# A two-layer diffusion backbone: earlier first weights, convolution reads at another priority, square sums through PSUM

## The chip, the cores and the metric

The kernel runs on one core of one Trainium2 chip. The metric is the device time of one execution in microseconds (us), as the median of several runs. TensorE (PE) multiplies, VectorE (DVE), ScalarE (ACT) and GpSimd (POOL) do the rest, and SyncE (SP) issues the transfers from and to HBM. Matrix products land in PSUM, in banks of 128 partitions x 512 fp32 numbers; everything else lives in SBUF.

## The reference, cut to what matters

The latent stream `x` has 512 tokens, the context 256, each token 1024 numbers; there are two layers. Each layer normalises its input, modulates it by a condition (`w_ada`), sends it through four mixers side by side, merges these, and ends with a SwiGLU FFN. The context is written out by the first layer only.

```python
mod_l = (silu_c @ w_ada[l] + b_ada[l])[:, None, :]
sh1, sc1, g1, sh2, sc2, g2 = jnp.split(mod_l, 6, axis=-1)
h_lat = modulate(rms_norm(x, norm1_g[l]), sh1, sc1)
h_ctx = modulate(rms_norm(h_ctx_stream, norm1_g[l]), csh1, csc1)
p_lat = h_lat @ lp['w_in']      # S5, SGU, SSD, latent attention, gates
p_ctx = h_ctx @ lp['w_in']
...
# latent attention: the low-rank q (384) and kv (256) are normalised per token
q = rms_norm(cq, lp['mla_q_a_norm']) @ lp['mla_w_uq']
kv = rms_norm(ckv, lp['mla_kv_a_norm']) @ lp['mla_w_ukv']
...
# SSD: a centred depthwise convolution of three taps over the tokens, then silu
xbc = jax.nn.silu(conv_centred(xbc, lp['ssd_conv_w'], lp['ssd_conv_b']))
...
x = x + g1 * mix_lat
x = x + g2 * swiglu(modulate(rms_norm(x, norm2_g[l]), sh2, sc2), w_ffn_in[l], w_ffn_out[l])
```

## The kernel before

Activations lie transposed: 128 features on the partitions, tokens along the row (768: 256 of the context, `CTXS`, and 512 latent, `LAT`). A product in fp32 is made of three products of halves: `split` lets ACT round a value to its high half (`whi`, `xh`, `hh`) and POOL or VectorE subtract to get the low half (`wlo`, `xl`, `hl`), and `mm3` multiplies high by low, high by high and low by high into one bank. `weights` loads 256 columns of a matrix by one transfer into a `raw` tile and splits them 128 at a time; there are two buffers each of `raw`, `whi` and `wlo`. `proj` takes such a pair of weights, runs the eight blocks of 128 features (24 products for one segment) into an `acc` bank, of which there are two, and hands the bank to a callback that reads it on ACT or VectorE.

*The start.* `run` issues the transfers for `x`, then by `ada_first` those for the first eight chunks of the modulation: 16 tiles `h` of 384 KB and 8 tiles `f` of 256 KB (the last quarter), then the context, then the first weights of `w_in` (`first = next(ws)`, with the casts). It transposes the latent tokens, norms them, multiplies the modulation chunks (`ada_chunk`: products with the condition `cT`, a copy `gs`, a transpose, a sum), and lets `norm_mod` write `h` for the latent tokens. `next(xt)` transposes the context, the second `next(norm)` norms it: squares on ACT, their sum on VectorE, a product with `ones` that sums over the features, a reciprocal root in about ten small steps on VectorE, a product that spreads the result over the partitions, and the modulated `h` of the context. Then `params_more` and `s5_scalars` prepare small parameters. `mix` begins with two projections (128 columns each of q's low-rank part): both over the latent tokens, then both over the context.

*The heads.* `mla_pair` handles 256 tokens of q (three blocks of features, `nk` = 3) or kv (`nk` = 2): load, split, the squares on ACT into an SBUF tile `sc`, their sum by one or two adds on VectorE, then `tok_rsqrt` (the product with `ones`, four instructions of 128 columns for 256 tokens, and a root), the products of the heads, a norm of each head and its rotation, and transposes (`b<-k,g`). It runs eleven times, six in layer 0 and five in layer 1, beside generators of the state-space layer.

*The convolution.* A callback of `conv` reads a bank three times: ACT multiplies by the middle tap, VectorE adds the two neighbours by two `scalar_tensor_tensor` instructions. It runs within `fill`, between the steps of attention.

*What sets the order.* Nobody writes an engine's order out: a scheduler sorts the instructions of all engines by priority, which is the order of the program shifted by `high_priority(offset)`, by data and by free buffers. `at(fill, -1000)` puts the projections of `fill` 1000 places back, `five` runs 300 ahead. Each engine then works its own queue strictly in that order, and so does SP's for its transfers. PSUM's eight banks are `acc` (2), `b1` (4) and `b5` (2); both of the last are called `b` in the rows. The helpers give the lines: L169 and L171 are ACT, L174 `tensor_tensor` on VectorE or POOL, L186 and L190 VectorE, L193 a product, L197 a transpose, L481 a copy.

Of the kernel before, what the change touches and what calls it, by code (L numbers as in the profile page):

```python
# [13 lines left out]
AF = mybir.ActivationFunctionType  # L14
ALU = mybir.AluOpType
# [4 lines left out]
P = 128  # L20
# [6 lines left out]
BR = 384  # L27
# [13 lines left out]
C_CQ = 2188  # L41
# [44 lines left out]
class Net:  # L86
# [311 lines left out]

    def ada_first(s, l):

        src = s.t["w_ada"][l].rearrange("(k p) f -> p k f", p=P)
        out = []
        for pool, tag, c, w, cuts in ((s.hp, "h", 0, 768, (0, 512, 768)), (s.hp, "h", 768, 768, (0, 256, 768)), (s.fp, "f", 1536, 512, (0, 512))):
            rows = []
            for k in range(KD):
                raw = pool.tile([P, w], F32, tag=tag, name=s.nm(tag))
                s.dma.dma_start(out=raw, in_=src[:, k, c:c + w])
                rows.append(raw)
            for a, b in zip(cuts, cuts[1:]):
                out.append(((c + a) // 256, b - a, [x[:, a:b] for x in rows]))  # L410
        return out

# [234 lines left out]
    def mla_pair(s, part, q, kd, off, t0, b0, xd, nk, nw, wh, wl, qk):  # L647
# [7 lines left out]
        s.split(xh, xl, x)  # L655
        sq, z = s.sc(), s.sc()
        s.act(sq, x[:, 0:2].rearrange("p k t -> p (k t)"), AF.Square)
        s.add(sq[:, :256], sq[:, :256], sq[:, 256:])
        if nk == 3:
            s.act(z[:, :256], x[:, 2], AF.Square)  # L660
            s.add(sq[:, :256], sq[:, :256], z[:, :256])
        r = s.tok_rsqrt(sq, 2, 1.0 / (nk * P), eps)
# [621 lines left out]

    def mix(s, l, q, xs, xd, hh, hl, segs, rest, ws):

# [13 lines left out]
        def to_dram(d, segs_, f=None):  # L1300
            y = s.gs()

            def cb(ps, off, n, v):
                (f or s.act)(y[:, off:off + n], ps)
                if off == segs_[-1][0]:
                    s.spill(d[:, off:], y[:, off:])
            return cb
# [11 lines left out]
        ws = ws or s.weights(w_in, C_CQ, BR)  # L1319
        pair = [(next(ws), to_dram(dq[c * P:(c + 1) * P], segs)) for c in range(2)]  # L1320
        for sg in segs:
            for w, cb in pair:
                s.proj(w, hh, hl, [sg], cb)
        s.proj(next(ws), hh, hl, segs, to_dram(dq[2 * P:BR], segs))
        next(load, None)
# [52 lines left out]
        def conv(c, segs_):  # L1378
# [3 lines left out]
            def cb(ps, off, n, v):  # L1382
                a = y[:, off:off + n]
                s.act(a, ps, AF.Identity, scale=w(1), bias=q["cb"][:, c:c + 1])
                s.stt(a[:, 1:n], ps[:, 0:n - 1], w(0), a[:, 1:n], ALU.mult, ALU.add)
                s.stt(a[:, 0:n - 1], ps[:, 1:n], w(2), a[:, 0:n - 1], ALU.mult, ALU.add)
                z = s.sc()[:, :n]
# [74 lines left out]

    def layer(s, l, q, f, xs, hh, hl, xd, extra, rest, late, then, ws=None):
        full = l < DEPTH - 1
        segs = [LAT, CTXS] if full else [LAT]
        yd, gd = s.mix(l, q, xs, xd, hh, hl, segs, rest, ws)
        mh, ml = s.merge(l, yd, gd, segs)
# [71 lines left out]
    def run(s):  # L1539
# [3 lines left out]
        xr = s.load_x()  # L1543
        chunks = s.ada_first(0)
        xr = s.load_ctx() + xr
        ws = s.weights(s.t["w_in"][0], C_CQ, BR)
        first = next(ws)
        q = turn({})
# [32 lines left out]
        next(norm)  # L1581
        next(xt)
        next(norm)
        s.params_more(0, q)
        L8 = 21
        s.s5_scalars()
        ex = prepare()
# [9 lines left out]

        s.layer(0, q, a["f"], xs, hh, hl, xd, ex, rest(a, 8, L8), rest(a, L8, 24), then, chain([first], ws))
        xd = [s.dram(f"x1_{k}", [P, TOK]) for k in range(KD)]
# [34 lines left out]
```

## Time and profile before

| | us |
|---|---|
| median of 3 runs | 2734.05 |
| lowest, highest | 2726.58, 2735.45 |
| the profiled execution | 2746.22 |
| its span in the trace | 2744.4 |
| TensorE busy | 2614.2 |
| VectorE, POOL, ACT busy | 1390.6, 1217.3, 959.9 |
| mean granted clock of TensorE, of 1 | 0.978 |

The profile is of one execution. The page begins with each engine's busy time, and goes on with slices of the span, the costliest groups of instructions, and what an engine's idle time was ended by. A table of stretches gives the same for any piece of the span, with the clock that TensorE was granted: 1.00 is 2.4 GHz, 0.50 is 1.2 GHz. The list in order of time shows single instructions, with the idle time before them in brackets and the instruction that ended it.

### The profile page before, as it was taken

The numbers are of one execution on the slowest core, as the hardware profiler recorded it, in microseconds if no ns is written. First come the engines' busy times: TensorE is split into PE (matmuls) and PEld (weight loads), VectorE is DVE, ScalarE is ACT, GpSimd is POOL, SyncE is SP. The second block draws the span as 40 slices with busy tenths as digits, with TensorE's granted clock in tenths as the row PEclk, the third lists the DMA queues.
The fourth block names the chain that finished last, engine by engine and source line by source line (L and its number), as shares of the span: only waits on it lengthen the run. The fifth ranks groups of instructions, "written<-read, shape, count | busy, mean of one in ns | idle before, by whom it ended". The sixth has DMA issues, their size and how long they took to land. (4 is left out here: it accounts for less than half of the span.)

```text
span 2744.4 us, 39887 instructions
## 1 busy us (share of the span) xinstructions
PE 2614.2 (95%) x14964; PEld 2136.0 (78%) x14964; DVE 1390.6 (51%) x2944; ACT 959.9 (35%) x1901; POOL 1217.3 (44%) x877
## 2 busy tenths in 40 slices
PE   7998999998999989999999989999999999899999
PEld 4787777777888877888888877887766877678887
DVE  6667777656535666552221243666647454421111
ACT  4244455552222233222222234445543233322222
POOL 3255544424433746563423334543224545444443
PEclk9999999999999999999999999999999999899999
DMA  7656645644446553442321334665544565333332
GB/s 254 179 177 196 193 149 164 193 124 149 141 145 215 174 164 118 119 123 71 100 78 55 100 103 156 195 194 179 154 145 151 183 191 188 92 111 93 101 99 77
DMA packets 426039, 397.31 MB, mean 145 GB/s; under 512 B 53092, under 2 KB 372248, under 8 KB 425752
## 3 DMA queue, kind: packets, MB, share of 16 engines
q1 hardware_dynamic: 425848, 394.78, 46.4%
q8 instruction: 118, 1.93, 0.3%
q14 instruction: 73, 0.60, 0.1%
HBM read 305.66 MB, written 89.05 MB: 144 GB/s over the span
## 5 line engine op out<-in xcount | busy, mean ns | idle before, releaser
L174 POOL TENSOR_TENSOR wlo<-raw,whi 128x1024 fp32r<-128x1024 f32 (+2 forms) x314 | 630.1, 2008 | 1040.9 <-ACT whi L169 995.4
L193 PE MATMUL acc<-h,whi 128*128 128x512 f32 (+2 forms) x3496 | 1043.4, 368 | 14.3 <-DVE gs L186 6.7
L193 PE MATMUL acc<-h,wlo 128*128 128x512 f32 (+2 forms) x2060 | 760.1, 369 | 11.7 <-POOL wlo L174 6.5
L193 PEld LDWEIGHTS acc<-h,whi 128*128 128x128 f32 (+1 forms) x3496 | 625.1, 190 | 127.8 <-issue 15.4
L169 ACT CAST whi<-raw 128x1024 fp32r<-128x1024 f32 (+2 forms) x390 | 324.9, 834 | 759.7 <-PE b L193 319.4
L193 PEld LDWEIGHTS acc<-h,wlo 128*128 128x128 f32 (+1 forms) x2060 | 390.9, 190 | 83.7 <-POOL wlo L174 11.7
L193 PE MATMUL acc<-g,whi 128*128 128x512 f32 (+1 forms) x768 | 244.8, 390 | 13.2 <-DVE g L186 6.3
L193 PE MATMUL acc<-f,whi 128*128 128x512 f32 (+1 forms) x600 | 230.6, 394 | 6.4 <-POOL f L174 6.1
L193 PE MATMUL b<-h,whi 128*128 128x256 f32 (+1 forms) x696 | 220.8, 326 | 0.0
L193 PE MATMUL b<-h,wlo 128*128 128x256 f32 (+1 forms) x660 | 216.1, 327 | 3.0 <-POOL wlo L174 3.0
L193 PE MATMUL b<-g,whi 128*128 128x256 f32 (+1 forms) x768 | 197.3, 334 | 1.9 <-ACT whi L169 1.9
L193 PE MATMUL b<-f,whi 128*128 128x256 f32 (+1 forms) x600 | 186.6, 321 | 1.7 <-ACT whi L169 1.7
L193 PE MATMUL b<-g,g 128*64 128x128 f32 (+5 forms) x915 | 183.7, 354 | 0.4 <-DVE g L190 0.3
L193 PEld LDWEIGHTS acc<-g,whi 128*128 128x128 f32 x768 | 139.6, 190 | 43.0 <-ACT whi L169 8.4
L193 PEld LDWEIGHTS b<-g,whi 128*128 128x128 f32 x768 | 136.3, 193 | 24.3 <-ACT whi L169 4.7
L193 PEld LDWEIGHTS b<-g,g 128*128 128x128 f32 (+2 forms) x915 | 124.2, 183 | 24.8 <-issue 14.7
L193 PEld LDWEIGHTS b<-h,whi 128*128 128x128 f32 x696 | 132.0, 191 | 13.5 <-issue 0.2
L186 DVE SCALAR_TENSOR_TENSOR sc<-sc,acc 128x512 f32<-128x512 f32 (+1 forms) x45 | 30.7, 682 | 220.3 <-ACT sc L171 220.3
L193 PEld LDWEIGHTS b<-h,wlo 128*128 128x128 f32 x660 | 126.3, 191 | 16.0 <-POOL wlo L174 4.6
L193 PEld LDWEIGHTS acc<-f,whi 128*128 128x128 f32 x600 | 113.0, 189 | 30.9 <-POOL f L174 7.6
L174 POOL TENSOR_TENSOR g<-sc,g 128x256 fp32r<-128x256 f32 (+2 forms) x81 | 86.6, 1070 | 113.7 <-ACT g L169 86.0
L193 PE MATMUL acc<-g,wlo 128*128 128x512 f32 (+1 forms) x336 | 131.4, 391 | 1.1 <-DVE wlo L174 0.7
(273 smaller groups left out, 3858.5 us busy)
## 6 DMA issues: line engine op xcount, KB each, us to landing
raw<-in_w_in_dram SPq DMA_DIRECT2D x50, 1024.0 KB
raw<-in_w_ffn_in_dram SPq DMA_DIRECT2D x88, 512.0 KB
raw<-in_w_ada_dram SPq DMA_DIRECT2D x40, 1024.0 KB
raw<-in_w_ffn_out_dram SPq DMA_DIRECT2D x36, 512.0 KB
gate<-gs SPq DMA_DIRECT2D x32, 384.0 KB
f<-s5w SPq DMA_DIRECT2D x48, 256.0 KB
raw<-in_w_branch_dram SPq DMA_DIRECT2D x32, 384.0 KB
gs<-gate SPq DMA_DIRECT2D x32, 384.0 KB
```

The costliest lines, as they stand in the source:

```text
L169: s.nc.scalar.copy(out=out, in_=x)
L174: (e or s.nc.vector).tensor_tensor(out=out, in0=a, in1=b, op=op)
L186: s.nc.vector.scalar_tensor_tensor(out=out, in0=a, scalar=sc, in1=b, op0=op0, op1=op1)
L193: s.nc.tensor.matmul(out=out, lhsT=l, rhs=r, start=start, stop=stop)
```

## The change

1. In `run`, the first transfer of `w_in` and its casts are asked for within `ada_first`, ahead of the `f` tiles. The context's transposes, its norm and `params_more` become a callback `ctx`, which `mix` calls after the first weights' latent projection; `s5_scalars` comes after the pair's projections. The second weights' latent projection follows the callback, then the two context projections.
2. The three reads of a convolution bank get `high_priority(2000)`, which within `fill` (-1000) makes +1000.
3. In `mla_pair` the square of the first block goes to SBUF (`z`), that of the second to a PSUM bank (`p`), a third one to SBUF; VectorE adds into `p` and writes the sum to SBUF, so that each add has one operand in SBUF and one in PSUM. ACT makes one square of 256 columns per block, where one of 512 took two blocks.

```diff
-    def ada_first(s, l):
+    def ada_first(s, l, between):
...
             rows = []
+            if tag == "f":
+                done = between()
             for k in range(KD):
...
-        return out
+        return out, done
...
-        sq, z = s.sc(), s.sc()
-        s.act(sq, x[:, 0:2].rearrange("p k t -> p (k t)"), AF.Square)
-        s.add(sq[:, :256], sq[:, :256], sq[:, 256:])
+        sq, z, p = s.sc(), s.sc(), s.b1()
+        s.act(z[:, :256], x[:, 0], AF.Square)
+        s.act(p[:, :256], x[:, 1], AF.Square)
         if nk == 3:
-            s.act(z[:, :256], x[:, 2], AF.Square)
-            s.add(sq[:, :256], sq[:, :256], z[:, :256])
+            s.act(z[:, 256:], x[:, 2], AF.Square)
+            s.add(p[:, :256], p[:, :256], z[:, 256:])
+        s.add(sq[:, :256], p[:, :256], z[:, :256])
...
-        pair = [(next(ws), to_dram(dq[c * P:(c + 1) * P], segs)) for c in range(2)]
-        for sg in segs:
+        pair = []
+        for c in range(2):
+            pair.append((next(ws), to_dram(dq[c * P:(c + 1) * P], segs)))
+            s.proj(pair[c][0], hh, hl, segs[:1], pair[c][1])
+            if c == 0 and ctx:
+                ctx()
+        for sg in segs[1:]:
             for w, cb in pair:
                 s.proj(w, hh, hl, [sg], cb)
+        if l == 0:
+            s.s5_scalars()
...
-                s.act(a, ps, AF.Identity, scale=w(1), bias=q["cb"][:, c:c + 1])
-                s.stt(a[:, 1:n], ps[:, 0:n - 1], w(0), a[:, 1:n], ALU.mult, ALU.add)
-                s.stt(a[:, 0:n - 1], ps[:, 1:n], w(2), a[:, 0:n - 1], ALU.mult, ALU.add)
+                with s.tc.high_priority(2000):
+                    s.act(a, ps, AF.Identity, scale=w(1), bias=q["cb"][:, c:c + 1])
+                    s.stt(a[:, 1:n], ps[:, 0:n - 1], w(0), a[:, 1:n], ALU.mult, ALU.add)
+                    s.stt(a[:, 0:n - 1], ps[:, 1:n], w(2), a[:, 0:n - 1], ALU.mult, ALU.add)
...
-        chunks = s.ada_first(0)
+        ws = s.weights(s.t["w_in"][0], C_CQ, BR)
+        chunks, first = s.ada_first(0, lambda: next(ws))
         xr = s.load_ctx() + xr
-        ws = s.weights(s.t["w_in"][0], C_CQ, BR)
-        first = next(ws)
...
         next(norm)
-        next(xt)
-        next(norm)
-        s.params_more(0, q)
+
+        def ctx():
+            next(xt)
+            next(norm)
+            s.params_more(0, q)
         L8 = 21
-        s.s5_scalars()
```

The order of the instructions on the engines shows what the scheduler makes of it. Tile numbers differ between the two kernels, names don't. First POOL at the start; `wlo` is the low half of the first weights, `h` the low halves of the latent input. Before:

```order
L1036 MEMSET g_851 128x48x4
L1059 MEMSET g_882 128x576
L174 TENSOR_TENSOR h_456<-sc_482,h_448 128x512
L1060 MEMSET g_883 128x576
L174 TENSOR_TENSOR wlo_198<-raw_195,whi_197 128x1024
L174 TENSOR_TENSOR wlo_1084<-raw_195,whi_1083 128x1024
L174 TENSOR_TENSOR h_457<-sc_486,h_449 128x512
```

After:

```order
L174 ISA
L174 TENSOR_TENSOR wlo_174<-raw_171,whi_173 128x1024
L1005 MEMSET f_937 128x48
L174 TENSOR_TENSOR wlo_731<-raw_171,whi_730 128x1024
L174 TENSOR_TENSOR h_450<-sc_458,h_442 128x512
L1010 MEMSET g_942 128x576
L1039 MEMSET g_994 128x48x4
L174 TENSOR_TENSOR h_452<-sc_466,h_444 128x512
L1039 MEMSET g_999 128x48x4
```

The two `wlo` stood behind all but one of POOL's six `h`, and stand ahead of all of them.

TensorE in the same stage; `b<-ones,sc` sums the context's squares over the features, `acc` are the latent projections of the pair. Before:

```order
L193 MATMUL acc_1088<-h_448,whi_197 128x512
L193 MATMUL acc_1088<-h_448,wlo_198 128x512
L193 MATMUL b_546<-ones,sc_522 128x128 x2
L193 MATMUL acc_1114<-h_442,wlo_1084 128x512
L193 MATMUL acc_1114<-h_451,whi_1083 128x512
L193 MATMUL acc_1114<-h_443,whi_1083 128x512
L193 MATMUL acc_1088<-h_457,whi_197 128x512
L193 MATMUL acc_1088<-h_449,whi_197 128x512
```

After; `b<-sc,ones` spreads the root, and the `acc` of the last rows is the first context projection:

```order
L193 MATMUL acc_735<-h_448,wlo_731 128x512
L193 MATMUL acc_735<-h_457,whi_730 128x512
L193 MATMUL acc_735<-h_449,whi_730 128x512
L193 MATMUL acc_735<-h_449,wlo_731 128x512
L193 MATMUL b_619<-ones,sc_595 128x128 x2
L193 MATMUL b_639<-sc_636,ones 128x256
L193 MATMUL acc_761<-h_450,whi_173 128x256
L193 MATMUL acc_761<-h_442,whi_173 128x256
```

The sum stood between the first and the second latent projection, and stands behind both, right ahead of the spreading product and the context projection.

VectorE at the last square sum of layer 1's heads, among work of the state-space layer (`f`). Before:

```order
L174 TENSOR_TENSOR f_17128<-f_17128,f_17105 128x384
L174 TENSOR_TENSOR f_17236<-f_17127,f_17129 64x4x95
L174 TENSOR_TENSOR sc_17143<-sc_17143 128x256
L174 TENSOR_TENSOR sc_17143<-sc_17143,sc_17144 128x256
L174 TENSOR_TENSOR f_17236<-f_17128,f_17130 64x4x95
L174 TENSOR_TENSOR f_17237<-f_17127,f_17129 64x4x95
L174 TENSOR_TENSOR f_17237<-f_17128,f_17130 64x4x95
L190 TENSOR_SCALAR ty_17152<-b_17149 128x2
```

After:

```order
L174 TENSOR_TENSOR f_17142<-f_17142,f_17119 128x384
L174 TENSOR_TENSOR f_17252<-f_17141,f_17143 64x4x95
L174 TENSOR_TENSOR b_17159<-b_17159,sc_17158 128x256
L174 TENSOR_TENSOR sc_17157<-b_17159,sc_17158 128x256
L174 TENSOR_TENSOR f_17252<-f_17142,f_17144 64x4x95
L174 TENSOR_TENSOR f_17253<-f_17141,f_17143 64x4x95
L174 TENSOR_TENSOR f_17253<-f_17142,f_17144 64x4x95
L190 TENSOR_SCALAR ty_17168<-b_17165 128x2
```

The two adds keep their place to one row, and now have a bank `b` among their operands.

TensorE in the mixing of layer 0 at the head transposes `b<-k,g`, behind the products of a modulation chunk (`acc<-raw,cT`). Before:

```order
L193 MATMUL acc_3579<-h_449,whi_3548 128x256
L193 MATMUL acc_3579<-h_449,wlo_3549 128x256
L193 MATMUL acc_3608<-raw_3606,cT 32x256 x8
L197 MATMUL b_2389<-k,g_2185 96x128 x3
L197 MATMUL b_2390<-k,g_2185 96x128 x3
L197 MATMUL b_2401<-k,g_2212 96x128 x3
L197 MATMUL b_2402<-k,g_2212 96x128 x3
L193 MATMUL acc_3631<-h_450,whi_3626 128x512
L193 MATMUL acc_3631<-h_442,whi_3626 128x512
```

After, with the same two transposes in the last rows, behind most of the products of the next projection:

```order
L193 MATMUL acc_3643<-h_448,whi_3638 128x512
L193 MATMUL acc_3643<-h_448,wlo_3639 128x512
L193 MATMUL acc_3643<-h_457,whi_3638 128x512
L197 MATMUL b_2314<-k,g_1964 96x128 x3
L197 MATMUL b_2315<-k,g_1964 96x128 x2
L197 MATMUL b_2444<-k,f_2434 128x128 x4
L197 MATMUL b_2452<-k,f_2436 128x128 x4
L197 MATMUL b_2315<-k,g_1964 96x128
L193 MATMUL acc_3643<-h_449,whi_3638 128x512
L193 MATMUL acc_3643<-h_449,wlo_3639 128x512
L197 MATMUL b_2395<-k,g_2191 96x128 x3
L197 MATMUL b_2396<-k,g_2191 96x128 x3
```

The transposes moved from ahead of this projection to its end.

TensorE a little later, at the start of a projection of the SGU input (`acc` over the 256 context tokens) whose bank a gelu has to free. Before:

```order
L193 MATMUL acc_3831<-h_457,whi_3826 128x512
L193 MATMUL acc_3831<-h_449,whi_3826 128x512
L193 MATMUL acc_3831<-h_449,wlo_3827 128x512
L197 MATMUL b_3024<-k,g_2676 96x128 x3
L197 MATMUL b_3025<-k,g_2676 96x128 x3
L197 MATMUL b_3042<-k,g_2699 96x128 x3
L197 MATMUL b_3043<-k,g_2699 96x128 x3
L193 MATMUL acc_3860<-h_450,whi_3826 128x256
L193 MATMUL acc_3860<-h_442,whi_3826 128x256
```

After, with products of the heads (`b<-g,g`) and transposes of the state-space layer ahead of it:

```order
L193 MATMUL b_2913<-g_2508,g_2858 128x384
L193 MATMUL acc_3843<-h_457,whi_3838 128x512
L193 MATMUL acc_3843<-h_449,whi_3838 128x512
L193 MATMUL acc_3843<-h_449,wlo_3839 128x512
L197 MATMUL b_2834<-k,f_2831 64x96 x4
L197 MATMUL b_2844<-k,f_2831 64x96 x4
L193 MATMUL acc_3872<-h_450,whi_3838 128x256
L193 MATMUL acc_3872<-h_442,whi_3838 128x256
L193 MATMUL acc_3872<-h_442,wlo_3839 128x256
L193 MATMUL acc_3872<-h_451,whi_3838 128x256
```

What stood ahead were transposes of an attention head; ahead now are products that came later before.

## Rows read from the trace of the kernel before

**Rows 1.** the page: busy us, share of the span, instructions, by engine

```profile
PE 2614.2 (95%) x14964; PEld 2136.0 (78%) x14964; DVE 1390.6 (51%) x2944; ACT 959.9 (35%) x1901; POOL 1217.3 (44%) x877
```

**Rows 2.** TensorE's waits: line <- releaser: us in total, times, longest

```profile
PE b L193 <- DVE sc L174: 9.9, 7, 2.6
PE b L197 <- DVE g L174: 4.5, 2, 3.2
```

**Rows 3.** stretches at the start: length, busy by engine, PEclk, DMA

```profile
0.00:25.00 25.00, 17.33 (x92) 9.96 (x92) 10.95 (x34) 9.99 (x22) 0.63 (x6) 1.00 0.91 348
33.00:64.00 31.00, 20.64 (x81) 14.42 (x79) 25.15 (x44) 15.74 (x31) 17.27 (x18) 0.83 0.55 181
```

**Rows 4.** TensorE in order of time: start, us, operation [idle <-releaser]

```profile
43.89 2.08 PE L193 MATMUL acc<-h,whi 128*128 128x512 f32 x4 [0.33 <-POOL h L174]
54.46 0.68 PE L193 MATMUL b<-ones,sc 128*128 128x128 f32 x4 [1.28 <-DVE sc L174]
60.71 0.60 PE L193 MATMUL b<-sc,ones 128*128 128x256 f32 x2
63.47 0.51 PE L193 MATMUL acc<-h,whi 128*128 128x256 f32 x2 [2.17 <-POOL h L174]
```

**Rows 5.** ACT, POOL, VectorE (DVE) in order of time, the start

```profile
42.72 1.98 ACT L169 CAST whi<-raw 128x1024 fp32r<-128x1024 f32 x2
...
44.33 4.75 POOL L174 TENSOR_TENSOR wlo<-raw,whi 128x1024 fp32r<-128x1024 f32 x2
49.05 1.32 POOL L174 TENSOR_TENSOR h<-sc,h 128x512 fp32r<-128x512 f32 x1
...
44.66 4.57 DVE L174 TENSOR_TENSOR rotq<-gnq,k 128x128 f32<-128x128 f32 x2
57.20 0.48 DVE L190 TENSOR_SCALAR sc<-k,ty 128x128 f32<-128x128 f32 x2
```

**Rows 6.** instruction groups: count | busy, mean ns | idle before, releaser

```profile
L174 DVE TENSOR_TENSOR sc<-sc 128x256 f32<-128x256 f32 x11 | 10.6, 964 | 7.0 <-ACT sc L171 7.0
L174 DVE TENSOR_TENSOR sc<-sc,sc 128x256 f32<-128x256 f32 x5 | 6.3, 1262 | 0.4
L174 DVE TENSOR_TENSOR b<-b,sc 128x256 f32<-128x256 f32 x18 | 7.7, 430 | 3.9 <-ACT sc L171 1.7 <-ACT b L171 1.2
...
L171 ACT ACTIVATE sc<-g 128x256 f32<-128x256 f32 x21 | 7.6, 407 | 9.0 <-DVE b L174 4.8 <-DVE mod L428 2.8 <-DVE g L186 1.3
```

**Rows 7.** VectorE, POOL, TensorE in order of time, layer 1's heads

```profile
1736.28 1.23 DVE L174 TENSOR_TENSOR sc<-sc 128x256 f32<-128x256 f32 x1
1737.61 2.40 DVE L174 TENSOR_TENSOR sc<-sc,sc 128x256 f32<-128x256 f32 x1
...
1737.19 2.53 POOL L174 TENSOR_TENSOR wlo<-raw,whi 128x1024 fp32r<-128x1024 f32 x1
...
1740.06 1.06 PE L193 MATMUL b<-ones,sc 128*128 128x128 f32 x4 [1.82 <-DVE sc L174]
```

**Rows 8.** stretches of the mixing, columns as in Rows 3

```profile
238.40:248.60 10.20, 5.67 (x29) 3.94 (x22) 9.99 (x14) 2.92 (x6) 9.33 (x7) 0.50 0.52 162
313.50:320.30 6.80, 5.68 (x13) 4.46 (x14) 6.59 (x17) 0.95 (x3) 6.31 (x5) 0.50 0.88 252
378.00:489.00 111.00, 110.35 (x738) 87.06 (x737) 84.17 (x186) 61.67 (x141) 52.22 (x40) 1.00 0.54 171
1740.30:1743.70 3.40, 3.40 (x17) 3.40 (x17) 2.98 (x13) 0.89 (x4) 0.00 (x0) 0.50 0.00 0
```

**Rows 9.** VectorE in order of time, layer 0's first pair

```profile
165.82 0.42 DVE L174 TENSOR_TENSOR sc<-sc,sc 128x256 f32<-128x256 f32 x1
```

**Rows 10.** TensorE in order of time, mixing of layer 0

```profile
237.92 1.52 PE L193 MATMUL acc<-raw,cT 128*32 128x256 f32 x16 [3.77 <-ACT gs L171]
...
308.40 0.51 PE L193 MATMUL acc<-h,whi 128*128 128x256 f32 x2 [2.33 <-DVE gs L186]
314.62 1.22 PE L193 MATMUL acc<-h,whi 128*128 128x512 f32 x2 [3.08 <-DVE gs L186]
```

More of the change, by code (lines that the diff above doesn't have):

```diff
@@ L1282, in s5_glu, with mix @@
             yield
-    def mix(s, l, q, xs, xd, hh, hl, segs, rest, ws):
+    def mix(s, l, q, xs, xd, hh, hl, segs, rest, ws, ctx):
         t = s.t
@@ L1461, in merge, with layer @@
         return mh, ml
-    def layer(s, l, q, f, xs, hh, hl, xd, extra, rest, late, then, ws=None):
+    def layer(s, l, q, f, xs, hh, hl, xd, extra, rest, late, then, ws=None, ctx=None):
         full = l < DEPTH - 1
         segs = [LAT, CTXS] if full else [LAT]
-        yd, gd = s.mix(l, q, xs, xd, hh, hl, segs, rest, ws)
+        yd, gd = s.mix(l, q, xs, xd, hh, hl, segs, rest, ws, ctx)
         mh, ml = s.merge(l, yd, gd, segs)
@@ L1596, in then @@
             next(nxt["norm"])
-        s.layer(0, q, a["f"], xs, hh, hl, xd, ex, rest(a, 8, L8), rest(a, L8, 24), then, chain([first], ws))
+        s.layer(0, q, a["f"], xs, hh, hl, xd, ex, rest(a, 8, L8), rest(a, L8, 24), then, chain([first], ws), ctx)
         xd = [s.dram(f"x1_{k}", [P, TOK]) for k in range(KD)]
```

## The prediction

> **What bounds the kernel.** I read the busy line of the page first: TensorE works 2614.2 of the 2744.4 us span, nearly twice as long as any other engine [rows 1]. So time is to be had only where TensorE waits, or runs at the lower of its two clock levels. Next come its waits, longest first in total; two entries are used here [rows 2]. Then the table of stretches, which puts the granted clock beside the busy time. The changed code runs in three places: the first 64 us, where TensorE is busy 20.64 of the 31 us from 33 to 64, at a mean clock of 0.83 [rows 3]; the token mixing of layer 0 (about 160 to 660 us); and that of layer 1 (about 1700 to 2240 us). There I looked up single waits in order of time. Merge and FFN in between keep their order on TensorE and are left alone.
>
> **Edit 1, first weights earlier.** Before, the first w_in product starts at 43.89 [rows 4]: ACT casts the weights only at 42.72, and POOL makes wlo from 44.33 to 49.08 [rows 5]. After, the transfer of the weights (1 MB) passes the eight of the modulation's last quarter and the four of the context on SP's queue, the casts stand ahead of all h on ACT, and both wlo ahead of h on POOL. The transfer takes 1.0486 MB / 348 GB/s = 3.0 us [rows 3], an estimate; the last modulation chunk, the h of k=4 to 7 that hang on it and the context rows come that much later. Ahead of it the queue carries 4 x 0.52 MB of x and 16 x 0.39 MB of modulation, 24 us at that rate; with 2 us of small ones, the 3.0 and the casts (1.98) wlo can begin at 31. Two wlo (4.75 together) and one h (1.32) on POOL [rows 5] end at 37.1, and with the seams between I put the first product at 38.5. The last h was made on POOL behind wlo, from 49.05 to 50.37 [rows 5]; without wlo in front, but 3.0 us later at its source, I put it at 47. At least twelve latent products follow. At 0.22 us each (25 in the 5.6 us from 55.14 to 60.71 [rows 4]) the latent pair ends between 50 (full clock) and 55 (much of it at half), against 60.71.
>
> What is late next is the context. Before, its square sum went to TensorE at 54.46, amid the latent products, and the reciprocal root on VectorE ended at 57.20 + 0.48 [rows 4, 5], under cover of products until 60.71. Now both products of the context norm stand behind all 48 latent ones. So TensorE stands through 57.68 - 55.14 = 2.5 us of root and 63.47 - 60.71 = 2.8 us of norm, with 1 us of small products between: 6.3 us from the end of the latent pair to the first context product. That product started at 63.47 and will at 56.3 to 61.3: 2 to 7 us gained. The new hole can cost a stretch at half clock, as the holes of this stage do in the row at 0.83; I charge 1 to 4 us. Net between +6 and -2; I take **2 us**, near the low end, since that row is the nearest. The S5 scalars, moved in the code, keep their place on VectorE: nothing.
>
> **Edit 3, square sums.** Sixteen adds with both inputs in SBUF took 10.6 + 6.3 = 16.9 us, mean 964 and 1262 ns; an add of that size with one input in PSUM takes 430 [rows 6]. VectorE loses 16.9 - 16 x 0.43 = 10.0 us, and ACT gains at most 11 x 0.407 = 4.5 [rows 6]; neither engine ends the span. TensorE waits for such a sum twice. At 1740.06 it waited 1.82; the two adds had taken 1.23 and 2.40 beside POOL's wlo, from 1737.19 to 1739.72 [rows 7]. At 0.43 each they end near 1737.1, before TensorE is free at 1738.24. The wait goes, and probably the half-clock stretch right behind it, 3.40 us of busy time [rows 8], half of which is 1.7. That is **3.5 us** (bounds 0 and 4.5). The other is the longest of its entry, 2.6 us near 166 [rows 2]: there the second add took 0.42 already [rows 9] and had stood behind VectorE's other work, as it still does. Nothing, within -0.6 and +0.5.
>
> A rule on this: the 2.40 us add ended 0.3 us after POOL's wlo [rows 7]. The Trainium skill, page "SBUF — State Buffer", section "Who interferes with whom", says that a VectorE instruction with two SBUF inputs waits for a whole GpSimd instruction that reads SBUF, and that one with a single SBUF input doesn't. The row agrees. The same rule speaks against edit 1, which puts both wlo beside the making of h; that is the second rival, worked out from rows.
>
> The added bank p is one of four that the pair's products and roots share. Where none is free ACT stands, and behind it in ACT's queue the copies that free TensorE's banks. The trace shows no such wait; the nearest is 3.77 us for ACT's gs at 237.92 [rows 10]. I take 0 and keep the loss for a rival.
>
> **Edit 2, convolution.** Reading the banks sooner can give TensorE only what it lacks there: it is busy 110.35 of 111 us from 378 to 489 [rows 8]. So +0.65 at most in layer 0. Against that, the reads now pass attention and state-space work on VectorE, at a price of one wait of the size at 314.62, 3 us [rows 10]. I take **0**, bounds +0.65 and -3.
>
> **What is displaced.** New priorities change the order of the whole mixing on TensorE. Four known waits of layer 0 change cover. The two for VectorE's g, ahead of the head transposes near 242, sum to 4.5 us [rows 2]; those transposes now follow almost all 24 products of the next projection, some 5.5 us of work, so 4.5 go. At 308.40 and 314.62 TensorE waits 2.33 and 3.08 for a gelu that has to free a bank [rows 10]; now products of the heads stand ahead of and inside the projection between. At best 5.41 us go, and half of the 5.68 that it was busy at half clock in the stretch behind [rows 8]: 8.25; I take 6.5. The wait at 237.92 stays, since the same rows stand ahead of it, and so the half clock from 238.40. Sum **11 us**.
>
> A new order brings new waits where there were none: in the full stretch from 378 there is nothing to win and all to lose. I bound them by zero and by three of the size at 237.92 with its half clock, 3.77 + 5.67 / 2 = 6.6 each [rows 8, 10], 20 us together, and take one, **7 us** rounded up.
>
> **Sum.** 2 + 3.5 + 0 + 11 - 7 = 9.5 us faster. The profiled execution took 2746.22 us (1.8 more than its span), 12.2 above the median of 2734.05. By its own time the sum is 2736.7; carried to the median, 2724.5.
>
> **Rivals.** *Displacement even:* new waits take all of the 11 us. Only the 5.5 of start and square sum remain: 2728.5. For it: priorities moved the order, not aim at these waits, and the stretch from 378 was full. Against: the known waits visibly have more work ahead of them.
>
> *Contention at the start:* two 128x128 products on VectorE took 4.57 us beside wlo at 44.66 [rows 5]. If the low halves of h on VectorE come 4.75 us late beside the moved wlo, the gain of 2 becomes a loss of 2.75: 2729.3. Against: VectorE makes two of eight low halves, in a stage that waits for transfers anyway. This is what the rule of the Trainium skill above would make of edit 1.
>
> *Slower, banks in the heads:* p finds no free bank, ACT stands, the gs copies behind it are late. A pair so hit costs TensorE 6.6 us, as at 237.92. Eleven pairs run; three take 19.8 us against gains of 16.5, from where on it is slower than before, and five give 2734 - 16.5 + 33 = 2750.5. For it: ACT's queue cost 3.77 us once already. Against: ACT works 35% of the span [rows 1], and a pair holds p for about a microsecond.
>
> *Edit 2 does nothing* is the value taken, and changes no time.
>
> **Chances.** A change of 0.3%, 8.2 us, is about the least that can be told from none. Faster by more, the forecast: 0.46. Within 0.3%: displacement even 0.25, contention 0.09. Slower: 0.20, by the banks from four pairs on (2744), or with all terms at their low ends together. The range: at best 6 + 4.5 + 0.65 + 12.75 = 23.9 us faster with no new wait, about 2710; at the other end 2742, which is 24.5 us of new waits against the 16.5. So 2709 to 2742 leaves out some 0.2, nearly all above. The likeliest case alone: 2709 to 2726.
>
> **What would show it.** Right: the first w_in product before 40 and the first context product before 61.5; no wait for a square sum near 1740, and no such add above 0.7 us; the waits of VectorE's g near 242 and of the gelu near 308 gone or under 1 us. Wrong: more than 7 us between latent and context products; ACT's squares among what TensorE waits for; new waits between 375 and 660. If these new ones pass 10 us in sum, the forecast falls.

## The result

The changed kernel takes 2754.59 us (median of 5 runs, 2744.65 to 2760.39), before 2734.05: slower by 0.77%, ratio 1.0077 with a 95% interval of 1.0058 to 1.0095. The forecast was 2724.5, faster, in a range up to 2742; its direction and its range were wrong.

The profiled execution took 2758.93 us, its span is 2757.1. The busy line of the page after, against [rows 1]:

```profile
PE 2622.5 (95%) x14964; PEld 2133.7 (77%) x14964; DVE 1399.8 (51%) x2944; ACT 959.7 (35%) x1912; POOL 1216.1 (44%) x877
```

TensorE is busy 8 us longer, and VectorE 9 us longer, although VectorE's square sums were to give back 10. To find the place I cut both traces at the same products, the n-th product of a projection with `whi`, so that a stretch holds the same work in both. Table of stretches (its columns are those of [rows 3]), first the kernel before, then after; the stretch begins behind the first six blocks of 128 columns of `w_in` and ends early in the merge:

```profile
118.45:748.80 630.35, 602.43 (x3932) 493.69 (x3930) 422.43 (x951) 276.16 (x640) 289.42 (x223) 0.98 0.55 168
```

```profile
114.64:761.16 646.52, 608.15 (x3931) 495.82 (x3929) 428.66 (x956) 276.21 (x646) 285.80 (x223) 0.98 0.54 164
```

| the same products of TensorE | before | after | difference |
|---|---|---|---|
| start to the cut at 118.45 / 114.64 | 118.45 | 114.64 | -3.8 |
| mixing of layer 0, to 748.80 / 761.16 | 630.35 | 646.52 | +16.2 |
| merge and FFN, to 1718.47 / 1730.91 | 969.67 | 969.75 | +0.1 |
| mixing of layer 1, to 2315.62 / 2328.34 | 597.15 | 597.43 | +0.3 |
| the rest of the span | 428.8 | 428.8 | 0 |

In this pair the start gained, and the mixing of layer 0 lost four times as much. In that stretch the idle time ahead of TensorE's instructions is 646.52 - 608.15 = 38.4 us, before 630.35 - 602.43 = 27.9: 10.5 of the 16.2 us are waits, and 5.7 are products that follow each other more slowly, at the same mean clock (0.98).

The pair is one execution of each kernel, and its spans are 12.7 us apart where the medians are 20.5 apart: the execution before was 12 us above its median, the one after 4. Two rows of the table read otherwise beside the traces of the experiments below, cut at the same products. In layer 1, six more traces whose products stand in the order of before take 588.6 to 592.2 us, and the five whose products stand in the order of after (this one among them) take 597.1 to 603.0. So edit 3 loses some 8 us there too, which the row of +0.3 hides, because the execution before took long in this stage. One trace of each, e1_start and v_layer1:

```profile
1711.82:2300.43 588.61, 568.07 (x3279) 441.00 (x3278) 355.70 (x778) 248.76 (x525) 264.57 (x196) 0.99 0.57 177
1712.51:2311.11 598.60, 574.78 (x3280) 440.64 (x3279) 367.77 (x778) 247.88 (x529) 265.95 (x196) 0.99 0.56 175
```

And the 3.8 us of the start are not all edit 1's: fifteen traces without it reach the first cut at 110.2 to 118.9 us (middle value 116.1), five with it at 112.4 to 115.4 (middle value 114.6).

**The waits that were to go.** TensorE, VectorE in order of time, mixing of layer 0 of the kernel after:

```profile
229.97 1.07 PE L193 MATMUL acc<-raw,cT 128*32 128x256 f32 x16 [1.43 <-ACT gs L171]
235.55 1.51 PE L197 MATMUL b<-k,g 128*96 128x128 f32 x6 [4.51 <-POOL g L174]
...
313.75 0.50 PE L193 MATMUL acc<-h,whi 128*128 128x256 f32 x2 [1.57 <-DVE gs L186]
322.20 1.22 PE L193 MATMUL acc<-h,whi 128*128 128x512 f32 x2 [5.32 <-DVE gs L186]
...
313.83 1.49 DVE L174 TENSOR_TENSOR g<-kd,ty 128x192 f32<-128x192 f32 x2
316.71 1.80 DVE L174 TENSOR_TENSOR g<-g,ty 128x384 f32<-128x384 f32 x2
318.91 0.68 DVE L186 SCALAR_TENSOR_TENSOR gs<-gs,acc 128x512 f32<-128x512 f32 x1
319.51 1.78 DVE L174 TENSOR_TENSOR f<-f,f 128x512 f32<-128x512 f32 x1
321.48 0.67 DVE L186 SCALAR_TENSOR_TENSOR gs<-gs,acc 128x512 f32<-128x512 f32 x1
```

The waits of 3.20 and 1.33 for VectorE's g (together the 4.5 of [rows 2]) are replaced by one of 4.51 for POOL's g at the same spot: other head transposes now stand right behind the modulation chunk. In place of 2.33 and 3.08 for the gelu's bank [rows 10] stand 1.57 and 5.32, and the VectorE rows tell why: the `gs` at 318.91 and 321.48, of which the latter ends right before TensorE goes on, come behind steps of a head's rotation (`g<-kd,ty`, `g<-g,ty`). Before, these stood behind the gelu:

```profile
313.89 0.67 DVE L186 SCALAR_TENSOR_TENSOR gs<-gs,acc 128x512 f32<-128x512 f32 x1
...
317.42 1.47 DVE L174 TENSOR_TENSOR g<-kd,ty 128x192 f32<-128x192 f32 x2
```

The list of TensorE's waits in this stretch, after:

```profile
PE acc L193 <- DVE gs L186: 10.5, 7, 5.3
PE b L193 <- DVE f L174: 8.5, 5, 3.5
PE acc L193 <- ACT gs L171: 4.6, 2, 3.2
PE b L197 <- POOL g L174: 4.5, 1, 4.5
```

Before:

```profile
PE acc L193 <- DVE gs L186: 6.7, 5, 3.1
PE b L193 <- DVE f L481: 4.0, 1, 4.0
PE b L193 <- DVE f L174: 3.9, 3, 1.8
```

So the gelu's bank is the longest entry of both lists, but its 3.8 us more are only a part of the 10.5.

**The start**, kernel after, TensorE, VectorE and POOL:

```profile
40.61 1.11 PE L197 MATMUL b<-k,gs 128*128 128x128 f32 x4 [3.62 <-ACT gs L169]
42.02 1.20 PE L193 MATMUL acc<-h,whi 128*128 128x512 f32 x2
55.77 0.71 PE L193 MATMUL b<-ones,sc 128*128 128x128 f32 x4 [0.41 <-DVE sc L174]
62.12 0.80 PE L193 MATMUL acc<-h,whi 128*128 128x256 f32 x2 [2.29 <-POOL h L174]
...
31.64 2.47 DVE L174 TENSOR_TENSOR mod<-mod,prma 128x8 f32<-128x8 f32 x3
34.15 2.27 DVE L186 SCALAR_TENSOR_TENSOR gs<-mod,prma 128x8 f32<-128x8 f32 x1
...
31.63 2.39 POOL L174 TENSOR_TENSOR wlo<-raw,whi 128x1024 fp32r<-128x1024 f32 x1 [30.47 <-DMA f<-in_w_ada_dram]
34.05 2.35 POOL L174 TENSOR_TENSOR wlo<-raw,whi 128x1024 fp32r<-128x1024 f32 x1
```

The first w_in product comes at 42.02 and the first context product at 62.12, where it was 43.89 and 63.47 [rows 4]. VectorE's small steps of the modulation (128x8) took 2.47 us for three and 2.27 for one beside POOL's wlo: the long one of the three (2.32) and the single one each ended 0.02 us after a wlo. In e1_start, below, the same steps came just ahead of POOL's first wlo, at 31.6, and took 0.30 and 0.17; its first w_in product was there at 38.44:

```profile
30.39 0.30 DVE L174 TENSOR_TENSOR mod<-mod,prma 128x8 f32<-128x8 f32 x3
30.73 0.17 DVE L186 SCALAR_TENSOR_TENSOR gs<-mod,prma 128x8 f32<-128x8 f32 x1
```

This is the contention that the second rival named, at other instructions than it named; the changed kernel still reaches the first cut as early as e1_start (114.64 and 114.60).

**The square sums.** The last one of layer 1, VectorE and TensorE of the kernel after, then the groups of adds and the costliest group beside them:

```profile
1748.72 0.41 DVE L174 TENSOR_TENSOR b<-b,sc 128x256 f32<-128x256 f32 x1
1749.17 0.42 DVE L174 TENSOR_TENSOR sc<-b,sc 128x256 f32<-128x256 f32 x1
...
1750.52 0.61 PE L193 MATMUL b<-ones,sc 128*128 128x128 f32 x4
...
L174 DVE TENSOR_TENSOR b<-b,sc 128x256 f32<-128x256 f32 x23 | 9.9, 428 | 6.8 <-ACT sc L171 4.2 <-ACT b L171 1.8
L174 DVE TENSOR_TENSOR sc<-b,sc 128x256 f32<-128x256 f32 x14 | 5.9, 420 | 6.1 <-ACT b L171 5.6
L174 DVE TENSOR_TENSOR f<-f,f 64x380 f32<-64x380 f32 x48 | 42.5, 886 | 5.0 <-POOL f L174 3.0 <-POOL f L1230 1.0
```

The two adds take 0.41 and 0.42, and the wait of 1.82 [rows 7] is gone. The sixteen adds stand in these two groups, whose means are 428 and 420 ns, as forecast. But VectorE's total did not fall: the group `f<-f,f 64x380`, unchanged, went from 711 to 886 ns on the mean, 34.2 to 42.5 us. Before:

```profile
L174 DVE TENSOR_TENSOR f<-f,f 64x380 f32<-64x380 f32 x48 | 34.2, 711 | 6.5 <-POOL f L174 3.9 <-POOL f L1227 1.8
```

These have two inputs in SBUF as well. The mean misleads here: most of the 48 take 0.55 us in both traces, and what grew is the number of those above 0.7 us, from seven to eleven (in layer 1 from three to eight). Each of them, in both traces, ended within 0.7 us of the end of a POOL instruction. In the six traces with edit 3 in layer 1 the mean of the group is 834 to 908 ns, in the fourteen others 632 to 757.

Near 166 the square sum no longer is what ends a wait, and yet nothing is gained. TensorE and ACT before:

```profile
166.30 0.86 PE L193 MATMUL b<-ones,sc 128*128 128x128 f32 x4 [2.58 <-DVE sc L174]
...
161.71 0.58 ACT L171 ACTIVATE gs<-acc 128x512 f32<-128x512 f32 x1
164.73 0.50 ACT L169 COPY ty<-ty 64x64 f32<-64x64 f32 x2 [2.45 <-DVE ty L174]
```

TensorE, ACT and VectorE after:

```profile
162.12 1.19 PE L193 MATMUL acc<-raw,cT 128*32 128x256 f32 x12 [3.19 <-ACT gs L171]
...
161.08 0.50 ACT L169 COPY ty<-ty 64x64 f32<-64x64 f32 x2 [2.89 <-DVE ty L174]
161.48 0.59 ACT L171 ACTIVATE gs<-acc 128x512 f32<-128x512 f32 x1
...
156.95 3.84 DVE L174 TENSOR_TENSOR ty<-f,f 128x64 f32<-128x64 f32 x2 [4.17 <-DMA f<-s5bc]
```

ACT's `gs`, which frees TensorE's bank, stood ahead of ACT's `ty` copies and now stands behind them, and these wait for VectorE's `ty<-f,f`, 3.84 us for two instructions. A wait of 3.19 for ACT took the place of 2.58 for the sum.

**The added bank.** ACT writes the second square of each pair into p, eleven times:

```profile
L171 ACT ACTIVATE b<-st 128x256 f32<-128x256 f32 x11 | 4.1, 377 | 5.1 <-DVE g L190 4.9
205.87 0.39 ACT L171 ACTIVATE b<-st 128x256 f32<-128x256 f32 x1 [4.87 <-DVE g L190]
```

Once, at 205.87 in layer 0, ACT stood 4.87 us for it, until VectorE had read another bank (`g<-b,gain` on L190); elsewhere it hardly stood. TensorE has no wait from 196 to 216, so no `gs` copy behind it was late enough to matter there.

### The profile page after: what moved, and what is told of

Read it like the earlier page. It is cut to its first block, busy times and chain, and to the rows that moved or that the text cites. A ratio compares the mean times of both kernels' runs of the same rounds, so it can differ in the third digit from the quotient of the medians.

```text
span 2757.1 us, 39875 instructions
## 1 busy us (share of the span) xinstructions
PE 2622.5 (95%) x14964; PEld 2133.7 (77%) x14964; DVE 1399.8 (51%) x2944; ACT 959.7 (35%) x1912; POOL 1216.1 (44%) x877
```

## The experiments

Ratios are against the kernel before on the same chip; five rounds each. "Layer 0" is the mixing of layer 0 in one profiled execution, cut at the same products as above (630.35 before). The last column counts TensorE's products, transposes among them, ahead of the last product of the last pair's square sum in layer 0, in the scheduler's order: how late the heads come.

| kernel | median us | ratio (95% interval) | layer 0 | last sum |
|---|---|---|---|---|
| before | 2732 to 2734 | 1 | 630.4 | 1384 |
| after | 2754.59 | 1.0077 (1.0058 to 1.0095) | 646.5 | 1449 |
| e1_start | 2729.07 | 0.9988 (0.9979 to 0.9997) | 629.6 | 1384 |
| e2_conv | 2731.49 | 0.9999 (0.9986 to 1.0011) | 629.8 | 1384 |
| e12 | 2735.07 | 1.0010 (0.9998 to 1.0021) | 630.1 | 1384 |
| e3_squares | 2757.24 | 1.0091 (1.0078 to 1.0104) | 644.2 | 1449 |
| v_dummy | 2745.02 | 1.0056 (1.0039 to 1.0073) | 644.7 | 1480 |
| v_own_bank | 2736.84 | 1.0018 (1.0008 to 1.0029) | 630.0 | 1386 |
| v_layer1 | 2738.71 | 1.0023 (1.0014 to 1.0032) | 627.5 | 1384 |
| v_split | 2738.95 | 1.0034 (1.0021 to 1.0048) | 639.2 | 1379 |
| split_five260 | 2737.89 | 1.0018 (1.0004 to 1.0033) | 637.1 | 1379 |
| n_five290 | 2734.63 | 1.0004 (0.9990 to 1.0017) | 629.0 | 1384 |
| n_five260 | 2730.66 | 0.9996 (0.9982 to 1.0009) | 635.7 | 1384 |
| n_fill1100 | 2727.64 | 0.9980 (0.9966 to 0.9994) | 627.0 | 1384 |
| e3_five260 | 2747.30 | 1.0059 (1.0044 to 1.0073) | 638.4 | 1449 |
| e3_fill1100 | 2749.79 | 1.0073 (1.0055 to 1.0092) | 643.7 | 1449 |
| m_late100 | 2748.84 | 1.0055 (1.0040 to 1.0069) | 646.5 | 1442 |
| e3_ahead400 | 2736.42 | 1.0005 (0.9994 to 1.0015) | 622.9 | 1366 |
| e1_own_bank | 2735.46 | 1.0010 (0.9998 to 1.0021) | 627.5 | 1386 |
| e1_fill1100 | 2731.52 | 0.9997 (0.9984 to 1.0011) | 630.0 | 1384 |

The five traces whose products in layer 0 stand in the order of before (before, e1_start, e2_conv, e12, v_layer1) give 627.5 to 630.4 there, so a difference of 5 us is more than one execution's chance.

### Which edit

**e1_start**, edit 1 alone:

```diff
-        chunks = s.ada_first(0)
+        ws = s.weights(s.t["w_in"][0], C_CQ, BR)
+        chunks, first = s.ada_first(0, lambda: next(ws))
...
-        next(xt)
-        next(norm)
-        s.params_more(0, q)
+        def ctx():
+            next(xt)
+            next(norm)
+            s.params_more(0, q)
... (`mix` as in the changed kernel)
```

> The kernel before with edit 1 alone (first weights earlier). The traces put the first 100 us of the changed kernel 3.8 us ahead of before, and this edit leaves VectorE's order in the mixing as it was but for 13 of 2946 instructions. If the start's gain is real and lasts: 2726 to 2732, some 3 to 4 us under before, and the start looks as in the changed kernel. If the loss of the whole change comes from the start (a later context, transfers out of step): 2745 or more.

**e2_conv**, edit 2 alone:

```diff
+                with s.tc.high_priority(2000):
                     s.act(a, ps, AF.Identity, scale=w(1), bias=q["cb"][:, c:c + 1])
... (the two `stt` likewise)
```

> The kernel before with edit 2 alone (convolution reads at normal priority). It moves 29 of VectorE's 2946 instructions, in layer 1. If the reads push the gelu's and attention's work back and so made the waits for gs in layer 0, 2740 to 2755. If it does nothing, as I took it: within 3 us of before, 2731 to 2737.

**e3_squares**, edit 3 alone:

```diff
-        s.act(sq, x[:, 0:2].rearrange("p k t -> p (k t)"), AF.Square)
-        s.add(sq[:, :256], sq[:, :256], sq[:, 256:])
+        s.act(z[:, :256], x[:, 0], AF.Square)
+        s.act(p[:, :256], x[:, 1], AF.Square)
... (the rest as in the changed kernel)
```

> The kernel before with edit 3 alone (square sums through PSUM). It alone moves 591 of VectorE's instructions and nearly the whole of what the full change moves. If the loss of 16 us between 160 and 750 us is this edit's: 2750 to 2762, slower than the whole change by the start's 3 to 4 us, with the waits for gs at 310 to 400 in its trace. If the loss belongs to the start or the convolution: about 2725 to 2731, the 3.5 us of the last square sum under before.

**e12**, edits 1 and 2 (both diffs above, without the third).

> Edits 1 and 2 without 3. If edit 3 made the loss: the start's gain stays, 2726 to 2733. If edits 1 and 2 disturb the mixing between them: 2740 or more.

Edit 3 alone is slower by 0.91%, more than the whole change; edit 1 alone is faster by 3.3 us (2732.42 to 2729.07), and no effect of edit 2 shows. e12 came out at 1.0010, above what its parts give (0.9988 and 0.9999); its layer 0 is as before, and where those 5 us arise wasn't followed up. The loss is edit 3's: 14 to 16 us of it lie in layer 0, where edit 2 leaves the products in the order of before, and some 8 in layer 1.

### What in edit 3

**v_own_bank**: the sums still go through PSUM, in the free half of the bank that `tok_rsqrt` takes anyway (its diff against edit 3, cut).

```diff
-        s.act(p[:, :256], x[:, 1], AF.Square)
+        s.act(p[:, 256:], x[:, 1], AF.Square)
...
-        r = s.tok_rsqrt(sq, 2, 1.0 / (nk * P), eps)
+        r = s.tok_rsqrt(sq, 2, 1.0 / (nk * P), eps, p)
```

> Edit 3 without its added bank: the second block's square and the adds use the free half of the bank in which the root's product lands later. The adds have a PSUM operand as in edit 3; VectorE's order in the mixing of layer 0 is that of before but for 57 instructions, in layer 1 it changes. If the loss came from the added bank and the order it makes: 2726 to 2737. If it came from the adds or squares through PSUM themselves: 2750 to 2760, as edit 3 alone (2757).

**v_split**: two squares for one, all in SBUF.

```diff
-        s.act(sq, x[:, 0:2].rearrange("p k t -> p (k t)"), AF.Square)
+        s.act(sq[:, :256], x[:, 0], AF.Square)
+        s.act(sq[:, 256:], x[:, 1], AF.Square)
```

> The kernel before with ACT's square of 512 columns cut into two of 256, everything in SBUF, no bank added. It moves 213 to 240 of VectorE's instructions in the first layer's heads, in another way than edit 3. If a bank is what costs: within 4 us of before, 2728 to 2736. If any new order of layer 0 loses against this one: 2738 to 2755.

**v_dummy**: the kernel before with a bank taken and hardly used.

```diff
-        sq, z = s.sc(), s.sc()
+        sq, z, p = s.sc(), s.sc(), s.b1()
+        s.act(p[:, :1], x[:, 0, :1])
+        s.act(z[:, 256:257], p[:, :1])
```

> The kernel before with a bank taken in each pair and only touched (one column copied in and out by ACT, two small copies more); squares and adds stay in SBUF. If the added bank is the cause, whatever is in it: 2745 to 2760. If the adds through PSUM are: within 5 us of before, 2728 to 2738.

**v_layer1**: edit 3 for layer 1 only (`if s.layer_no == 1:` around it, the old lines else).

> Edit 3 in layer 1 only. Layer 0 keeps its order to the instruction. If the loss is all in layer 0, as the times between the two traces say, and the last square sum's 3.5 us are real: 2727 to 2733. If layer 1 loses too: 2736 or more.

The same stretch of layer 0 in the two that part bank and sums, own bank first:

```profile
116.14:746.17 630.03, 606.02 (x3931) 495.78 (x3930) 415.03 (x952) 277.46 (x646) 285.90 (x223) 0.97 0.54 168
```

```profile
116.23:760.89 644.66, 609.45 (x3931) 496.66 (x3929) 426.95 (x952) 276.95 (x652) 288.14 (x223) 0.98 0.53 164
```

The sums through PSUM with no bank added cost layer 0 nothing; the bank with the old sums costs it 14 us. So neither the adds nor the squares in PSUM are the loss there. v_dummy's 14 us do not come from the gelu's bank: that entry of its list is 6.7 us, as before, and VectorE's f rose from 3.9 to 11.1:

```profile
PE b L193 <- DVE f L174: 11.1, 6, 3.5
```

VectorE is busy 1367.5 us in all with the own bank, 23 less than before, and the kernel is not faster for it. v_split was the odd one: no bank, no PSUM, and 9 us lost. Layer 1 loses some 6 us by edit 3 too (v_layer1, whose products in layer 0 stand as before), though its wait for the last square sum is gone.

### Bank or order

A bank more per pair changes the scheduler's order; so do other small edits. Three kernels change one number of the priorities and no instruction.

**n_five290**, **n_five260** and **n_fill1100**:

```diff
-        five = at(state_space(), 300)
+        five = at(state_space(), 290)
...
-        fill = at(fill, -1000)
+        fill = at(fill, -1100)
```

> The kernel before with one number changed: the state-space work runs 290 places ahead of the program instead of 300. Not one instruction is added, removed or given other operands; the scheduler's order changes, by 148 of VectorE's 2946 instructions. If the bank or the PSUM adds as such cost the time: within 3 us of before, 2729 to 2736. If the order of before is simply better than a changed one: 2737 to 2750, with the mixing of layer 0 longer than 630 us at the same products.

> The same with 260 instead of 300: 190 of VectorE's instructions change place, most of them in the first layer's heads. Bank or PSUM: 2729 to 2736. Order: 2737 to 2755, and layer 0's mixing 635 to 646 us.

> The kernel before with the fill of attention (convolution, z) set back 1100 places instead of 1000: 75 of VectorE's instructions move, behind the heads. Bank or PSUM: 2729 to 2736. Order: 2734 to 2745.

My theory that the order of before is just better than any other fell here: the three lie between 0.9980 and 1.0004, one of them even faster than before. None of them moves the last pair's sum. n_five260's trace has a longer layer 0 all the same (635.7); its execution is the longest of twelve (2739.79), and the median shows no loss.

**e3_five260** and **e3_fill1100** give edit 3, **split_five260** gives v_split, another order by the same numbers (their diffs are the two above together).

> Edit 3 with the state-space work 260 instead of 300 places ahead; 167 of VectorE's instructions move against edit 3 alone, the heads stay as late as there (last pair's sum at product 1449, before 1384). Bank theory: 2750 to 2765, layer 0's mixing 640 us or more. Bad draw: anywhere between 2730 and 2760, layer 0 630 to 645.

> Edit 3 with the fill set back 1100 instead of 1000 places; 24 of VectorE's instructions move. Without edit 3 this change gave 5.5 us. Bank theory: 2748 to 2760, layer 0 640 us or more. Bad draw: may fall to 2735 to 2745.

> The cut squares in SBUF, no bank, with 260 instead of 300. Bank theory: the 9 us that the cut lost in layer 0 were its draw, and another draw gives 627 to 640 there, 2728 to 2740 in all. If two squares for one cost ACT, and so TensorE, something at any order: layer 0 again 637 to 643, 2737 to 2745.

All five kernels so far that take the bank in layer 0 (after, e3_squares and v_dummy too) lose, 0.56 to 0.91%; it isn't one bad draw. v_split keeps most of its loss in layer 0 (637.1 in split_five260) in another draw.

But all with the bank also have late heads. The last two take that apart. **m_late100** sets the heads of layer 0 back and changes nothing else; **e3_ahead400** is edit 3 with the heads pulled ahead:

```diff
-        drain(s.mla(l, q, dq, kd, segs, qk), five, 2)
+        drain(at(s.mla(l, q, dq, kd, segs, qk), -100) if l == 0 else s.mla(l, q, dq, kd, segs, qk), five, 2)
```

(400 in place of -100 in the second.)

> The kernel before with layer 0's heads set back by 100 places of priority, nothing else: no bank, squares as before. The last pair's sum moves from product 1384 to 1435, as late as with edit 3 (1449). If the late heads cost: layer 0's mixing 638 to 648 us, 2740 to 2752. If the bank costs by itself: 626 to 634 us, 2728 to 2736.

> Edit 3 with layer 0's heads set 400 places ahead: bank and PSUM sums stay, the last pair's sum comes at 1366. If the late heads cost: layer 0 back to 626 to 634 us, and 2737 to 2742, with what layer 1 loses (6 us) left. If the bank costs by itself: 638 us or more, 2746 to 2760.

Layer 0's mixing, m_late100 first, with TensorE's longest wait there, VectorE ahead of it, and the entry of the gelu's bank:

```profile
117.59:764.08 646.49, 606.71 (x3931) 497.95 (x3930) 435.93 (x951) 276.13 (x640) 287.06 (x223) 0.97 0.54 164
...
318.66 1.22 PE L193 MATMUL acc<-h,whi 128*128 128x512 f32 x2 [8.56 <-DVE gs L186]
...
311.21 2.77 DVE L174 TENSOR_TENSOR g<-kd,ty 128x192 f32<-128x192 f32 x2
314.44 1.82 DVE L174 TENSOR_TENSOR g<-g,ty 128x384 f32<-128x384 f32 x2
317.93 0.67 DVE L186 SCALAR_TENSOR_TENSOR gs<-gs,acc 128x512 f32<-128x512 f32 x1
...
PE acc L193 <- DVE gs L186: 9.7, 2, 8.6
```

and e3_ahead400:

```profile
111.83:734.76 622.93, 599.33 (x3931) 489.95 (x3930) 417.30 (x957) 276.54 (x646) 286.57 (x223) 0.99 0.55 170
```

Late heads without a bank cost layer 0 as much as edit 3 does (646.5 us; 1.0055 in all, since the products of layer 1 stay in the order of before; the execution is the longest of six). The longest wait is again that for the gelu's bank, 8.56 us behind the rotation of a late head. In sum, though, that entry rose only from 6.7 to 9.7 us, while all of TensorE's idle time there rose from 27.9 to 39.8; the rest is spread over other waits. Edit 3 with early heads has the shortest layer 0 of all, 622.9, and no loss against before shows.

So for layer 0, late heads are enough for the whole loss, and edit 3 with early heads doesn't have it: edit 3 lost there by what its bank did to the place of the heads in the order. That the bank as such is free isn't shown by this. With its heads early, e3_ahead400 also has none of the wait of ACT for p (the square that waited 4.87 us in the changed kernel waits under 0.1), and the kernel before with its heads 400 ahead, the counterpart without a bank, was not run. No ACT square appears among what TensorE waits for.

Layer 1 closes the sum: 16 us of layer 0 and 8 of layer 1, less some 3 of the start, make the 20.5 between the medians, and in e3_ahead400 7 us won in layer 0 stand against some 8 lost in layer 1. Two things stay open: why v_split loses 7 to 9 us in layer 0 with its heads as early as before, and by what mechanism edit 3 costs layer 1 its 6 to 8 us. It isn't the bank alone: v_dummy has the bank there, in another order, and takes 581.1 us in its trace.

**e1_own_bank** and **e1_fill1100** put two parts together (their diffs stand above).

> Edit 1 with the square sums through the bank of the root's product (no bank added). If the parts add up: the start's 3 us under the own-bank kernel's 2737, that is 2732 to 2735, level with before. If the adds' freed time comes out once the start is shorter: under 2729, better than edit 1 alone.

> Edit 1 and the fill set back by 1100. If the two gains (3.3 and 5.5 us) belong to different places and add: 2722 to 2726, faster than both kernels. If the second is a draw that edit 1 undoes: 2727 to 2733.

Neither adds up: 1.0010 and 0.9997. Of the four pairs of kernels here that differ by edit 1 alone, two got faster by it (before to e1_start, v_own_bank 1.0018 to e1_own_bank 1.0010) and two slower (e2_conv 0.9999 to e12 1.0010, n_fill1100 0.9980 to e1_fill1100 0.9997). Gains of 3 to 5 us from two edits are each within what the next order gives or takes. Faster than both kernels by its interval are e1_start (0.9988, up to 0.9997) and n_fill1100 (0.9980, up to 0.9994); with eighteen kernels tried, one such interval can be chance. Edit 3 in layer 0 alone with early heads, and edit 1, was not run.

## Why the prediction was wrong

*Edit 1: right at the start, not shown for the whole time.* I took 2 us. The first context product stands at 59.5 to 62.1 in the five traces with edit 1 (middle value 60.6) and at 60.2 to 63.8 in the fifteen without (62.5), which is my 2 us. e1_start is 3.3 us faster in the median, but on two of four kernels edit 1 brought a loss, so what reaches the end depends on the order behind it. The first product at 42.02 missed my 40; alone, edit 1 had it at 38.44. ACT's first h began at 32.41 there and at 36.45 in the changed kernel, behind VectorE's small step of 2.27 us beside wlo. For the 6.3 us from the latent pair's end to the context product I measure 6.8 (the pair ends at 55.77 - 0.41), and that product came at 62.12 instead of before 61.5.

*Edit 2: right.* Nothing taken, nothing measured (0.9999, interval 0.9986 to 1.0011).

*Edit 3's sums: the step was right and its worth was not.* About 0.42 us per add as forecast, and the wait at 1740 gone in the changed kernel. But the 3.5 us didn't reach the time: v_layer1 is 6 us slower, so this term alone is some 10 us off. I had counted the gain at one wait and treated the order around it as given, since at that spot it was the same to one row; TensorE's order over the whole of layer 1's mixing is another.

*What is displaced: the failed step.* I took 11 us for waits that would go and charged 7 for new ones. Measured: +16.2 us for the mixing of layer 0, so 20 us off in this term alone. Both halves failed. Two of the known waits were not covered but handed on: I looked whether those same transposes and projections had more work ahead, and not what now stood in their old place. At the first, other transposes did, and TensorE waited 4.51 for 4.53. At the gelu, VectorE's queue decided, not TensorE's cover: the rotation of a late head stood ahead of the reads. And I charged the new waits by one known wait, where waits grew by 10.5 us net and the products' own pace by 5.7, a term that my sum had only as half clock behind a wait. I looked for the new waits from 378 on; from 375 to 660 the entries of the list of waits sum to 11.3 us after and 8.4 before, so most of the growth came ahead of that. Of the 30 us between forecast and result this term makes 20 and the square sums' term the other 10.

*The rivals.* "Banks in the heads" had the right edit and the right side, and its price for five pairs (2750.5) lies near the result, but that is luck: ACT stood for p once (4.87 us at 205.87), and TensorE didn't wait for what stood behind. I had taken that p finds its bank free, since a pair holds it for about a microsecond; from the square to the end of the last add it was 1.7 us at 205.87 and 5.4 us at 157.48. "Displacement even" named the right term, with too little. The range ended at 2742 because I let 24.5 us of new waits (by my own bound 20) stand against gains of 16.5, of which only the start's 2 came.

*The carrying to the median.* The profiled execution of before was 12 us over the median. Its waits of layer 0 recur in e1_start, e2_conv and e12 almost to the tenth (2.33 and 3.08 at the gelu again), so they were a fair base for layer 0. Of layer 1 the same products in the same order took 597.15 there and 588.6 in e1_start, so that stage of it was a poor one.

## What to carry to other kernels

Where a scheduler makes the order, an edit to a small helper is an edit to the order of all that follows: look where the moved chain now starts and ends (here the last pair's sum, product 1449 after 1384) before counting single waits. And don't call a stage unchanged on one pair of executions: layer 1's loss of some 8 us stood as 0.3 in the table until more traces were cut at the same products. A wait whose instruction moved is only gone if what now stands in its place is ready, and if the queue of the engine that releases it didn't change. And before an edit is blamed or praised for half a per cent, give the kernel before two or three orders that change no instruction; if they differ by as much, the edit's own worth hasn't been measured.

## What the runs showed of the hardware

I had not expected that relieving sixteen VectorE instructions of their waits for POOL would leave VectorE busier. The 10 us were made up by others: 8.4 us in the group `f<-f,f 64x380`, nearly all in layer 1, where eight instead of three instructions of the group took 0.9 to 2.7 us, and the others 0.55. So a saving of this kind can come back at other instructions with two SBUF inputs, and how much depends on the order; with the own bank, another order, VectorE's total fell by 23 us. And neither total moved the kernel's time. The rule of the Trainium skill ("SBUF — State Buffer", "Who interferes with whom") is that a VectorE instruction with two SBUF inputs contends with a POOL instruction that reads SBUF, and that one with at most one SBUF input does not (its modes that take both ports apart). For the single instruction the traces agree: in all twenty no add of 128x256 with one input in PSUM took over 0.44 us, while the adds of that size with both inputs in SBUF took 0.41 to 2.44 us in the kernel before.
